# The sums behind a norm move from GpSimd to ScalarE, the power ahead of the copies, and the last output goes out in quarters

## The chip, the cores and the metric

One core of one Trainium2 chip. The metric is the device time of one execution in microseconds (us), the median of several; less is better. The core has five engines with queues of their own: TensorE (PE; its weight loads are shown apart as PEld), VectorE (DVE), ScalarE (ACT), GpSimd (POOL) and SyncE (SP), which here issues DMA transfers. Each engine takes its instructions strictly in the order of its own queue, and waits at an instruction until what it needs from other engines is there.

## The reference

Four decoder layers on 256 rows of 1024 columns, float32. In layers 0 and 3 the mixer is differential attention, in layer 1 stick-breaking attention, in layer 2 sliding-window attention. Each sublayer has a norm ahead of it and one behind it, and the one behind is what is changed here:

```python
def rms_norm(x, g):
    y = xf * lax.rsqrt(jnp.mean(xf * xf, axis=-1, keepdims=True) + NORM_EPS)
    return (y * g.astype(jnp.float32)).astype(x.dtype)
...
for i in range(DEPTH):
    hn = rms_norm(x, norm_gains[i, 0])
    m = mixer[i % 3](hn, ...)
    x = x + rms_norm(m, norm_gains[i, 1])
    hn = rms_norm(x, norm_gains[i, 2])
    x = x + rms_norm(swiglu(hn, ffn_w_gate[i], ffn_w_up[i], ffn_w_down[i]), norm_gains[i, 3])
```

## The kernel before

**Streams and weights.** The 256 rows are two streams, s = 0 (rows 0 to 127) and s = 1 (rows 128 to 255), each with its running state `x` of 128x1024 in on-chip memory. Both go through the same weights, stream 1 some units behind stream 0. A unit of weights, 128x1024, comes by DMA into `stage`, is rounded by ScalarE into `hi`, and VectorE takes the rest, `lo` = `stage` − `hi`. Activations are split alike (`xh` and `xl` behind a norm, `hTh` and `hTl` in the FFN), and each product is three matmuls: hi·high, lo·high and hi·low. FFN sums go to `mm_f` (gate and up) and, behind the down projection, to `acc_f`; the mixers' to `acc_a`, `acc_b` and `acc_c`.

**FFN hidden.** VectorE makes a block `h_f` of 128x256; GpSimd copies it into two planes of 16-bit words (`hp_f`); a DMA turns it (`hq_f`); GpSimd puts the words together again (`words`, L574 to L576, tile `hx_f`); from that ScalarE makes `hTh_f` and VectorE `hTl_f`, which the matmuls into `acc_f` take.

**Norms.** `post_norm` (L458) works on a sublayer's two sums of 128x512: ScalarE squares each and adds its columns up (`junk` with the sum in a column of `ssp`), GpSimd takes `u` = first sum + epsilon + second sum (one instruction, a TENSOR_SCALAR) and `r` = u to the power −0.5, both in `rstd_of` (L394), 128x1 each; VectorE makes `mg` = sum × gain, and then `x` += `mg` × `r` in two halves of 128x512. Tiles are named `_m` behind a mixer and `_e` behind an FFN. The next `pre_norm` (tiles `_q` ahead of an FFN, `_n` ahead of a mixer) has TensorE turn `x` in eight blocks of 128x128 (`tp_q`, `tp_n`: two tiles of four), from which ScalarE makes `xh` and VectorE `xl`; ScalarE also squares `x` (`junk_q`), and GpSimd makes `u_q` and `r_q`, from which VectorE makes `half` and `hsq` for the FFN. Behind the last layer SP writes each stream's `x` in two halves (L952 to L954).

**What sets the order.** `Emitter` (L39) runs the two streams as generators, with a clock of estimated matmul times and with delays that are written as `yield ("d", ns)`; that gives the order in which instructions are emitted. In the start phase each is pinned to that order on its engine (`Start`, L182); once that phase is over `.on` is False, and a scheduler of the framework puts each engine's instructions in an order of its own, by what they need and by its estimates of time. Only what goes through `tc.keep_in_program_order` stays where it was emitted: from then on the loads of weights and gains. Since the helper `run` at L182 issues nearly all instructions, the profile shows them under L182, and tiles tell them apart; only a few instructions issued directly have lines of their own.

Of the kernel before, what the change touches and what calls it, by code (L numbers as in the profile page):

```python
# [9 lines left out]
F32 = mybir.dt.float32  # L10
# [3 lines left out]
U16 = mybir.dt.uint16  # L14
AF = mybir.ActivationFunctionType
ALU = mybir.AluOpType
# [3 lines left out]
P = 128  # L20
# [3 lines left out]
EPS = 1e-6  # L24
# [134 lines left out]
def trunk_kernel(ctx, tc, x, positions, norm_gains, a_w_in, a_w_out, a_lambda, a_subln, b_w_in, b_w_out,  # L159
                 c_w_in, c_w_out, c_sinks, w_gate, w_up, w_down, out, depth=DEPTH):  # L160
    nc = tc.nc
# [4 lines left out]
    sm = ctx.enter_context(tc.tile_pool(name="sm", bufs=2))  # L166
# [20 lines left out]
    act, dve, pool, pe = (Start(e) for e in (nc.scalar, nc.vector, nc.gpsimd, nc.tensor))  # L187
# [87 lines left out]
    xs = [cst.tile([P, D], F32, name=f"x_{s}") for s in range(2)]  # L275
# [12 lines left out]
    mhalf = sm.tile([P, 8], F32, name="mhalf", bufs=1)  # L288
# [54 lines left out]
    def scalars():  # L343

        yield ("d", 9000)
        lsum = sm.tile([P, 4], F32, tag="lsum", name="lsum", bufs=1)
        lprod = wk.tile([P, 4, 64], F32, tag="t2k", name="lprod", bufs=TMP)
        lv = lam_in.rearrange("p i a b d -> p (i a) b d")
        pool.tensor_tensor(lprod, lv[:, :, 0, :], lv[:, :, 1, :], ALU.mult)
        dve.tensor_reduce(lsum, lprod, AX.X, ALU.add)  # L350
        act.activation(lsum, lsum, AF.Exp)
        for j in range(2):
            pool.tensor_scalar(nlam[:, j:j + 1], lsum[:, 2 * j + 1:2 * j + 2], lsum[:, 2 * j:2 * j + 1], -lam_init[j],
                                    ALU.subtract, ALU.add)
        tc.keep_in_program_order(pool.tensor_scalar(nsink, nsink, -1.0, None, ALU.mult))
        tps = bank("tp", 1, [P, 2], "tp_sub")
        nc.tensor.transpose(tps, subr, ident[:2, :2])
        for j in range(2):
            dve.tensor_scalar(gsub[:, j:j + 1], tps[:, j:j + 1], 1.0 - lam_init[j], None, ALU.mult)
# [31 lines left out]
        pe.transpose(o, i, ident)  # L391
        em.t += P * COLUMN_NS * 4

    def rstd_of(name, s, ss, more=EPS, extra=None):  # L394

        u = sm.tile([P, 1], F32, tag=f"u{s}", name=f"u_{name}")
        r = sm.tile([P, 1], F32, tag=f"r{s}", name=f"r_{name}", bufs=3)
        pool.tensor_scalar(u, ss, more, extra, ALU.add, *([ALU.add] if extra else []))
        pool.tensor_tensor(r, u, mhalf[:, 0:1], ALU.pow)
        return r  # L400

    def pre_norm(s, n, name):
# [24 lines left out]
        def rms():  # L427
            if n == 0:
                yield ("d", 2500)
                if s == 0:  # L430
                    sines(*angles)
                else:
                    act.on = dve.on = pool.on = False
            junk = wk.tile([P, D], BF16, tag="junk", name=f"junk_{name}", bufs=1)
            act.activation(junk, xs[s], AF.Square, scale=1.0 / 32, accum_out=ss)
            xn[2] = rstd_of(name, s, ss)
# [16 lines left out]
    def gain_of(i, n):  # L453
        if (i, n) not in gain_tiles:
            gain_tiles[i, n] = load_gain(i, n)
        return gain_tiles[i, n]

    def post_norm(s, acc, gain, name):  # L458
        ss = sm.tile([P, 2], F32, tag=f"ssp{s}", name=f"ssp_{name}")
        junk = wk.tile([P, D], BF16, tag="junk", name=f"junk_{name}", bufs=1)  # L460
        mg = [wk.tile([P, 512], F32, tag="t2k", name=f"mg_{name}{h}", bufs=TMP) for h in range(2)]
        for h in range(2):
            act.activation(junk[:, h * 512:(h + 1) * 512], acc[h], AF.Square, scale=1.0 / 32, accum_out=ss[:, h:h + 1])
        r = rstd_of(name, s, ss[:, 0:1], ss[:, 1:2], EPS)
        for h in range(2):
            dve.tensor_tensor(mg[h], acc[h], gain[:, h * 512:(h + 1) * 512], ALU.mult)
        for h in range(2):
            cs = slice(h * 512, (h + 1) * 512)
            dve.scalar_tensor_tensor(xs[s][:, cs], mg[h], r, xs[s][:, cs], ALU.mult, ALU.add)

    def rows_product(acc, ah, al, w, first, last):

# [11 lines left out]
    def out_proj(s, oT, name, last):  # L484

        acc = None
        for kt in range(KT):
            yield ("e", (name, "o", kt))
            w = yield ("w",)
            if acc is None:  # L490
                yield ("e", (name, "s", last))
                acc = [bank("acc", s, [P, 512], f"acc_{name}_{h}") for h in range(2)]
            oh, ol = (t[:, kt % 4, :] for t in oT[kt // 4])
            rows_product(acc, oh, ol, w, kt == 0, kt == KT - 1)
        return acc
# [77 lines left out]

    def words(dst, turned):  # L574

        pool.tensor_copy(dst.bitcast(U16).rearrange("p b (t w) -> p w b t", w=2), turned)  # L576

    def two_groups(s, name):
        return [[wk.tile([P, 4, P], F32R, tag=f"o{p}{s}", name=f"o{p}_{name}{g}") for p in "hl"] for g in range(2)]
# [298 lines left out]
    def ffn(s, i, xn):  # L878
# [19 lines left out]
        def turn(c, h):  # L898
            yield ("d", 2600)
            turned = by_dma(h, 2, f"{name}{c}")  # L900
            yield ("d", 4200)
            if c % 2 == 0:
                hT[c] = hT[c + 1] = [wk.tile([P, 4, P], F32R, tag=f"o{q}{s}", name=f"hT{q}_{name}{c}") for q in "hl"]
            t = wk.tile([P, 2, P], F32, tag="t2k", name=f"hx_{name}{c}", bufs=TMP)
            words(t, turned)
            split_rows(hT[c], slice(2 * (c % 2), 2 * (c % 2) + 2), t)
            em.set((name, "h", c))
# [23 lines left out]
    def stream(s):  # L931
        if s:
            yield ("d", 1500)
        for i in range(depth):
            kind = i % 3
            xn = pre_norm(s, 4 * i, f"n{i}{s}")
            yield ("d", 600)
            if i == 0 and s:
                em.spawn(scalars())
            oT, name = yield from (layer_a, layer_b, layer_c)[kind](s, i, xn)  # L940
            gain = gain_of(i, 1)
            acc = yield from out_proj(s, oT, name, (1, 1, 3)[kind])
            post_norm(s, acc, gain, f"m{i}{s}")
            yield ("d", 4000)
            gain = gain_of(i, 3)
            xn = pre_norm(s, 4 * i + 2, f"q{i}{s}")
            yield ("d", 600)
            acc = yield from ffn(s, i, xn)
            post_norm(s, acc, gain, f"e{i}{s}")
            if i < depth - 1:  # L950
                yield ("d", 4000)
        for h in range(2):  # L952
            cs = slice(h * 512, (h + 1) * 512)
            nc.sync.dma_start(out[0, s * P:(s + 1) * P, cs], xs[s][:, cs])  # L954

    em.run([stream(0), stream(1)])


# [23 lines left out]
```

## Time and profile before

| | |
|---|---|
| median of 3 runs | 1188.16 us (1187.87 to 1189.1) |
| the profiled execution | 1188.83 us, of which the span from its first to its last instruction is 1187.0 us |
| clock granted to TensorE | 0.997 of full speed |
| busy: TensorE, VectorE, ScalarE, GpSimd | 98%, 66%, 55%, 19% of the span |
| moved by DMA | 216.41 MB, 182 GB/s over the span |
| splits of weights | 378 `hi` of 1058 ns each, 378 `lo` of 1225 ns each |
| copies of FFN words | 80 `hp_f` of 1139 ns, 80 `hx_f` of 996 ns |
| powers behind a mixer (`r_m`) | 8 of 574 ns; their `u_m` 8 of 303 ns |

A row of the timeline gives the start, the duration, the engine, the line, the operation, output<-inputs with partitions x elements and type, and how many like it in a row; in brackets the idle time of the engine just ahead of it and what ended it. A row of the waits gives who waited for whom, the us in total, the times and the longest. A row of the groups gives the count behind x, the busy us in total, the mean ns of one, and then the idle time ahead of them. Consecutive rows of one engine may overlap by about 0.1 us, since the next instruction begins before the last one's result is complete.

### The profile page before, as it was taken

The page shows a single profiled execution, that of the slowest core. Times are in us where ns is not written, and L with a number is a line of the kernel's source. Part 1 is how long each engine was busy: PE and PEld are TensorE (multiplying, and loading weights), DVE is VectorE, ACT ScalarE, POOL GpSimd, SP SyncE. Part 2 cuts the span into 40 slices and gives each one's busy share as a digit, 9 for nine tenths or more (in the row PEclk, how much of TensorE's full clock was granted, in tenths as well). Part 3 has the DMA queues.
Part 4 walks back from the last instruction along what each step waited for, and adds up shares of the span by engine and source line. Part 5 has one row for each costly group of instructions (what it writes and reads, how often), then busy time and mean ns, then how long its engine had stood idle before and what let it go on. Part 6 is the DMA issues. An engine that isn't in the chain of part 4 may idle for free.

```text
span 1187.0 us, 16749 instructions
## 1 busy us (share of the span) xinstructions
PE 1165.1 (98%) x5869; PEld 957.0 (81%) x5869; DVE 782.7 (66%) x1213; ACT 655.3 (55%) x1209; POOL 224.5 (19%) x319
## 2 busy tenths in 40 slices
PE   8999999999999999999999999999999999999997
PEld 6787788888878878888888878888888788888886
DVE  6876665665847666665688666666586775766563
ACT  6665654444756655444477655444475565544441
POOL 5100132222200013222210013222210001322221
PEclk9999999999999999999999999999999999999999
DMA  7635467776743646777664346877765364577761
GB/s 261 210 125 176 131 193 220 208 221 198 221 135 126 213 129 190 205 221 208 199 197 160 108 129 195 213 211 214 205 198 155 131 192 150 177 212 212 208 194 40
DMA packets 183948, 216.41 MB, mean 182 GB/s; under 512 B 52788, under 2 KB 148152, under 8 KB 183864
## 3 DMA queue, kind: packets, MB, share of 16 engines
q1 hardware_dynamic: 183716, 215.28, 60.9%
q8 instruction: 46, 0.75, 0.3%
q14 instruction: 38, 0.31, 0.1%
q10 hardware_dynamic: 148, 0.07, 0.0%
HBM read 203.76 MB, written 1.05 MB: 173 GB/s over the span
## 4 chain that ended last, share of the span: by engine, by line
PE 89%; DVE 3%; ACT 2%; issue 2%; POOL 2%; DMA 2%; DVEq 0%; POOLq 0%; ACTq 0%; SPq 0%
PE mm_f L182 39%; PE acc_f L182 18%; PE acc_a L182 3%; PE mm_c L182 2%; PE acc_b L182 2%; PE acc_c L182 2%; PE sc_a L182 1%; DVE lo L182 1%; PE sc_c L182 1%; ACT hi L182 1%; PE sc_b L182 1%; DVE x L182 1%; DMA stage<-in_a_w_in_dram 1%; PE pv_a L182 1%; PE mm_a000k L182 1%
## 5 line engine op out<-in xcount | busy, mean ns | idle before, releaser
L182 DVE TENSOR_TENSOR lo<-stage,hi 128x1024 fp32r<-128x1024 f32 x378 | 459.5, 1225 | 163.0 <-ACT hi L182 160.6
L182 ACT ACTIVATE hi<-stage 128x1024 fp32r<-128x1024 f32 x378 | 396.0, 1058 | 168.0 <-PE mm_f L182 87.5
L182 PE MATMUL mm_f<-hi,xh_q 128*128 128x512 f32 x704 | 275.4, 391 | 1.5 <-ACT hi L182 1.5
L182 PE MATMUL mm_f<-lo,xh_q 128*128 128x512 f32 x704 | 274.0, 389 | 0.0
L182 PE MATMUL mm_f<-hi,xl_q 128*128 128x512 f32 x704 | 217.1, 389 | 0.4 <-DVE xl_q L182 0.4
L182 POOL COPY hp_f<-h_f 128x512 uint16<-128x512 uint16 x80 | 91.1, 1139 | 411.7 <-DVE h_f L182 404.9
L182 PEld LDWEIGHTS mm_f<-hi,xh_q 128*128 128x128 f32 x704 | 132.1, 188 | 30.2 <-ACT hi L182 3.2
L182 PEld LDWEIGHTS mm_f<-hi,xl_q 128*128 128x128 f32 x704 | 132.1, 188 | 28.9 <-DVE xl_q L182 1.3
L182 PEld LDWEIGHTS mm_f<-lo,xh_q 128*128 128x128 f32 x704 | 132.2, 188 | 27.1
L182 ACT ACTIVATE hTh_f<-hx_f 128x256 fp32r<-128x256 f32 x80 | 33.5, 419 | 160.8 <-POOL hx_f L182 160.8
L182 PE MATMUL acc_f<-hi,hTh_f 128*128 128x512 f32 x352 | 111.5, 392 | 1.2 <-ACT hTh_f L182 1.2
L182 PE MATMUL acc_f<-hi,hTl_f 128*128 128x512 f32 x352 | 109.8, 389 | 0.0
L182 PE MATMUL acc_f<-lo,hTh_f 128*128 128x512 f32 x352 | 109.8, 389 | 0.0
L182 DVE TENSOR_TENSOR hTl_f<-hx_f,hTh_f 128x256 fp32r<-128x256 f32 x80 | 33.9, 424 | 100.9 <-ACT hTh_f L182 100.9
L182 POOL COPY hx_f<-hq_f 128x512 uint16<-128x512 uint16 x80 | 79.7, 996 | 82.6 <-DMA hq_f<-hp_f 82.3
L182 ACT ACTIVATE t_f<-mm_f,half_f 128x256 f32<-128x256 f32 x88 | 41.6, 473 | 77.4 <-PE mm_f L182 77.4
L182 PEld LDWEIGHTS acc_f<-hi,hTh_f 128*128 128x128 f32 x352 | 65.8, 188 | 15.6 <-ACT hTh_f L182 2.4
L182 PEld LDWEIGHTS acc_f<-lo,hTh_f 128*128 128x128 f32 x352 | 66.1, 188 | 13.9
L182 PEld LDWEIGHTS acc_f<-hi,hTl_f 128*128 128x128 f32 x352 | 66.0, 188 | 13.8
L182 DVE SCALAR_TENSOR_TENSOR t_f<-t_f,mm_f 128x256 f32<-128x256 f32 x88 | 36.8, 419 | 34.1 <-ACT t_f L182 33.9
L182 DVE SCALAR_TENSOR_TENSOR h_f<-t_f,hsq_f,mm_f 128x256 f32<-128x256 f32 x88 | 42.3, 480 | 2.9
L182 ACT ACTIVATE e_a<-sc_a,nm_a 128x128 f32<-128x128 f32 (+1 forms) x64 | 26.1, 421 | 16.4 <-DVE nm_a L182 16.3
(589 smaller groups left out, 1557.5 us busy)
## 6 DMA issues: line engine op xcount, KB each, us to landing
stage<-in_ffn_w_gate_dram SPq DMA_DIRECT2D x176, 256.0 KB, 3.0
stage<-in_ffn_w_up_dram SPq DMA_DIRECT2D x176, 256.0 KB, 3.3
stage<-in_ffn_w_down_dram SPq DMA_DIRECT2D x88, 512.0 KB, 4.4
stage<-in_a_w_in_dram SPq DMA_DIRECT2D x48, 512.0 KB, 4.4
stage<-in_b_w_in_dram SPq DMA_DIRECT2D x24, 512.0 KB, 3.8
stage<-in_a_w_out_dram SPq DMA_DIRECT2D x16, 512.0 KB, 3.7
stage<-in_c_w_in_dram SPq DMA_DIRECT2D x10, 512.0 KB, 3.8
gain<-in_norm_gains_dram SPq DMA_DIRECT2D x8, 512.0 KB, 5.8
```

Source lines behind the costliest of these rows:

```text
L182: i = call(*args, **kw)
```

## The change

`rstd_of` now serves `pre_norm` alone. In `post_norm` GpSimd adds epsilon to the first sum, in place, as soon as that is there; ScalarE adds the two sums (an Identity activation of the second sum with the first as bias); GpSimd then takes only the power. The power and the copy in `words` are issued through `keep_in_program_order`, so on GpSimd these two kinds stay in the order in which they were emitted; GpSimd's other instructions are placed by the scheduler as before. In the last layer's FFN `post_norm` the four quarters of `x` are made one by one, and each stream's output goes out as 512, 256 and 256 columns.

```diff
@@ -391,11 +391,11 @@
         pe.transpose(o, i, ident)
         em.t += P * COLUMN_NS * 4
 
-    def rstd_of(name, s, ss, more=EPS, extra=None):
+    def rstd_of(name, s, ss):
 
         u = sm.tile([P, 1], F32, tag=f"u{s}", name=f"u_{name}")
         r = sm.tile([P, 1], F32, tag=f"r{s}", name=f"r_{name}", bufs=3)
-        pool.tensor_scalar(u, ss, more, extra, ALU.add, *([ALU.add] if extra else []))
+        pool.tensor_scalar(u, ss, EPS, None, ALU.add)
         pool.tensor_tensor(r, u, mhalf[:, 0:1], ALU.pow)
         return r
 
@@ -455,18 +455,24 @@
             gain_tiles[i, n] = load_gain(i, n)
         return gain_tiles[i, n]
 
-    def post_norm(s, acc, gain, name):
+    def post_norm(s, acc, gain, name, width=512):
         ss = sm.tile([P, 2], F32, tag=f"ssp{s}", name=f"ssp_{name}")
         junk = wk.tile([P, D], BF16, tag="junk", name=f"junk_{name}", bufs=1)
         mg = [wk.tile([P, 512], F32, tag="t2k", name=f"mg_{name}{h}", bufs=TMP) for h in range(2)]
+        u = sm.tile([P, 1], F32, tag=f"u{s}", name=f"u_{name}")
+        r = sm.tile([P, 1], F32, tag=f"r{s}", name=f"r_{name}", bufs=3)
         for h in range(2):
             act.activation(junk[:, h * 512:(h + 1) * 512], acc[h], AF.Square, scale=1.0 / 32, accum_out=ss[:, h:h + 1])
-        r = rstd_of(name, s, ss[:, 0:1], ss[:, 1:2], EPS)
+            if h == 0:
+                pool.tensor_scalar(ss[:, 0:1], ss[:, 0:1], EPS, None, ALU.add)
+        act.activation(u, ss[:, 1:2], AF.Identity, bias=ss[:, 0:1])
+        tc.keep_in_program_order(nc.gpsimd.tensor_tensor(r, u, mhalf[:, 0:1], ALU.pow))
         for h in range(2):
             dve.tensor_tensor(mg[h], acc[h], gain[:, h * 512:(h + 1) * 512], ALU.mult)
         for h in range(2):
-            cs = slice(h * 512, (h + 1) * 512)
-            dve.scalar_tensor_tensor(xs[s][:, cs], mg[h], r, xs[s][:, cs], ALU.mult, ALU.add)
+            for c in range(0, 512, width):
+                cs = slice(h * 512 + c, h * 512 + c + width)
+                dve.scalar_tensor_tensor(xs[s][:, cs], mg[h][:, c:c + width], r, xs[s][:, cs], ALU.mult, ALU.add)
 
     def rows_product(acc, ah, al, w, first, last):
 
@@ -573,7 +579,7 @@
 
     def words(dst, turned):
 
-        pool.tensor_copy(dst.bitcast(U16).rearrange("p b (t w) -> p w b t", w=2), turned)
+        tc.keep_in_program_order(nc.gpsimd.tensor_copy(dst.bitcast(U16).rearrange("p b (t w) -> p w b t", w=2), turned))
 
     def two_groups(s, name):
         return [[wk.tile([P, 4, P], F32R, tag=f"o{p}{s}", name=f"o{p}_{name}{g}") for p in "hl"] for g in range(2)]
@@ -946,11 +952,10 @@
             xn = pre_norm(s, 4 * i + 2, f"q{i}{s}")
             yield ("d", 600)
             acc = yield from ffn(s, i, xn)
-            post_norm(s, acc, gain, f"e{i}{s}")
+            post_norm(s, acc, gain, f"e{i}{s}", 256 if i == depth - 1 else 512)
             if i < depth - 1:
                 yield ("d", 4000)
-        for h in range(2):
-            cs = slice(h * 512, (h + 1) * 512)
+        for cs in (slice(0, 512), slice(512, 768), slice(768, 1024)):
             nc.sync.dma_start(out[0, s * P:(s + 1) * P, cs], xs[s][:, cs])
 
     em.run([stream(0), stream(1)])
```

The instructions of the two kernels stand in the same order up to small places around each `post_norm`. Tiles have a running number behind the name, which the change shifts by a few (`hi_1601` before is `hi_1603` after).

GpSimd in layer 0, from the FFN copies of stream 0 around the post-norm of stream 1's mixer (`_m`) to its next pre-norm (`_q`), before and then after:

```order
L182 COPY hp_f_1525<-h_f_1489 128x512
L182 TENSOR_SCALAR u_m_1573<-ssp_m_1567 128x1
L182 COPY hx_f_1583<-hq_f_1527 128x2x256
L182 TENSOR_TENSOR r_m_1574<-u_m_1573,mhalf 128x1
L182 COPY hp_f_1605<-h_f_1594 128x512
L182 TENSOR_SCALAR u_q_1640<-ss_q_1609 128x1
L182 TENSOR_TENSOR r_q_1641<-u_q_1640,mhalf 128x1
```

```order
L182 COPY hp_f_1526<-h_f_1490 128x512
L182 TENSOR_SCALAR ssp_m_1568<-ssp_m_1568 128x1
L469 TENSOR_TENSOR r_m_1573<-u_m_1572,mhalf 128x1
L582 COPY hx_f_1585<-hq_f_1528 128x2x256
L182 TENSOR_SCALAR u_q_1642<-ss_q_1611 128x1
L182 TENSOR_TENSOR r_q_1643<-u_q_1642,mhalf 128x1
L182 COPY hp_f_1607<-h_f_1596 128x512
```

The power has changed places with the copy `hx_f`, and `u_q` and `r_q` with the copy `hp_f`. ScalarE at the same place, before and after:

```order
L182 ACTIVATE junk_m_1568,ssp_m_1567<-acc_a_0_1349 128x512
L182 ACTIVATE junk_m_1568,ssp_m_1567<-acc_a_1_1350 128x512
L182 ACTIVATE hi_1601<-stage_1512 128x1024
L182 ACTIVATE hTh_f_1581<-hx_f_1583 128x256
L182 ACTIVATE t_f_1593<-mm_f_1493,half_f_1426 128x256
L182 ACTIVATE xh_q_1610<-tp_q_0_1612,gains 128x128 x4
L182 ACTIVATE xh_q_1610<-tp_q_1_1617,gains 128x128 x4
L182 ACTIVATE junk_q_1638,ss_q_1609<-x_111 128x1024
```

```order
L182 ACTIVATE junk_m_1569,ssp_m_1568<-acc_a_0_1350 128x512
L182 ACTIVATE junk_m_1569,ssp_m_1568<-acc_a_1_1351 128x512
L182 ACTIVATE hi_1603<-stage_1513 128x1024
L182 ACTIVATE u_m_1572<-ssp_m_1568 128x1
L182 ACTIVATE t_f_1595<-mm_f_1494,half_f_1427 128x256
L182 ACTIVATE hTh_f_1583<-hx_f_1585 128x256
L182 ACTIVATE junk_q_1640,ss_q_1611<-x_111 128x1024
L182 ACTIVATE xh_q_1612<-tp_q_0_1614,gains 128x128 x4
L182 ACTIVATE xh_q_1612<-tp_q_1_1619,gains 128x128 x4
```

The add stands behind the weight split `hi`, and not directly behind the squares; `hTh_f` has gone behind `t_f`, and `junk_q` ahead of `xh_q`. TensorE there, from the first matmul with that `hi` on, before and after:

```order
L182 MATMUL mm_f_1685<-hi_1601,xh_q_1386 128x512
L182 MATMUL acc_f_0_1655<-hi_1538,hTh_f_1581 128x512
L182 MATMUL tp_q_0_1612<-ident,x_111 128x128 x4
L182 MATMUL acc_f_1_1656<-hi_1538,hTh_f_1581 128x512
L182 MATMUL tp_q_1_1617<-ident,x_111 128x128 x4
L182 MATMUL mm_f_1648<-hi_1299,xh_q_1610 128x512
```

```order
L182 MATMUL mm_f_1687<-hi_1603,xh_q_1387 128x512
L182 MATMUL acc_f_0_1657<-hi_1539,hTh_f_1583 128x512
L182 MATMUL acc_f_1_1658<-hi_1539,hTh_f_1583 128x512
L182 MATMUL acc_f_0_1657<-lo_1540,hTh_f_1583 128x512
L182 MATMUL acc_f_1_1658<-lo_1540,hTh_f_1583 128x512
L182 MATMUL tp_q_0_1614<-ident,x_111 128x128 x4
L182 MATMUL mm_f_1687<-lo_1604,xh_q_1387 128x512
L182 MATMUL tp_q_1_1619<-ident,x_111 128x128 x4
```

Four matmuls that take `hTh_f` now stand ahead of the first turn of `x`, where one stood. On VectorE the subtraction that belongs to that `hi` (`lo_1604`, before `lo_1602`) has moved from behind `t_f` to between `mg_m` and `x`, and the `xl_q` behind `half` and `hsq`. The other layers show the same moves; in layer 2 the kernel before had even the first `acc_f` behind `tp_q_0`.

Behind the FFN of stream 1 in layer 1, ScalarE after the change (before, the same rows without `u_e`, which was GpSimd's):

```order
L182 ACTIVATE junk_e_5951,ssp_e_5950<-acc_f_0_4659 128x512
L182 ACTIVATE hi_6221<-stage_6076 128x1024
L182 ACTIVATE junk_e_5951,ssp_e_5950<-acc_f_1_4660 128x512
L182 ACTIVATE hi_6280<-stage_6094 128x1024
L182 ACTIVATE u_e_5954<-ssp_e_5950 128x1
L182 ACTIVATE hi_6334<-stage_6169 128x1024
L182 ACTIVATE xh_n_6029<-tp_n_0_6031,gains 128x128 x3
```

The add stands behind a `hi` here too, in layers 0 to 2; TensorE and VectorE keep their orders at these places. Behind the last layer it stands directly behind its squares.

## The prediction

> **What bounds the kernel now.** First the page: the span, the busy time and the chain that ended last.
>
> ```profile
> span 1187.0 us, 16749 instructions
> PE 1165.1 (98%) x5869; PEld 957.0 (81%) x5869; DVE 782.7 (66%) x1213; ACT 655.3 (55%) x1209; POOL 224.5 (19%) x319
> PE 89%; DVE 3%; ACT 2%; issue 2%; POOL 2%; DMA 2%; DVEq 0%; POOLq 0%; ACTq 0%; SPq 0%
> ```
>
> TensorE sets the end: busy for 98% of the span, and 89% of the chain. The change touches no matmul, so it can only alter TensorE's pauses. Its waits, largest first, hold three groups that lie around a post-norm:
>
> ```profile
> PE tp_q L182 <- DVE x L182: 2.5, 4, 1.2
> PE mm_f L182 <- ACT hi L182: 1.5, 4, 0.4
> PE acc_f L182 <- ACT hTh_f L182: 1.2, 4, 0.5
> ```
>
> Each occurs four times: once a layer, where stream 1 leaves its mixer. The timeline of layer 0 there, ScalarE, GpSimd, VectorE and TensorE in turn:
>
> ```profile
> 142.51 0.20 ACT L182 ACTIVATION_READ_ACCUMULATOR junk_m<-acc_a 128x1 f32 x1
> 142.60 1.05 ACT L182 ACTIVATE hi<-stage 128x1024 fp32r<-128x1024 f32 x1
> 143.95 0.42 ACT L182 ACTIVATE hTh_f<-hx_f 128x256 fp32r<-128x256 f32 x1 [0.31 <-POOL hx_f L182]
> 142.80 0.30 POOL L182 TENSOR_SCALAR u_m<-ssp_m 128x1 f32<-128x1 f32 x1 [7.75 <-ACT junk_m L182]
> 143.16 0.76 POOL L182 COPY hx_f<-hq_f 128x512 uint16<-128x512 uint16 x1
> 143.85 0.57 POOL L182 TENSOR_TENSOR r_m<-u_m,mhalf 128x1 f32<-128x1 f32 x1
> 144.46 1.41 DVE L182 SCALAR_TENSOR_TENSOR x<-mg_m,r_m,x 128x512 f32<-128x512 f32 x2 [1.04 <-POOL r_m L182]
> 143.70 0.49 PE L182 MATMUL mm_f<-hi,xh_q 128*128 128x512 f32 x1 [0.37 <-ACT hi L182]
> 144.42 0.50 PE L182 MATMUL acc_f<-hi,hTh_f 128*128 128x512 f32 x1 [0.23 <-ACT hTh_f L182]
> 145.36 0.63 PE L182 MATMUL tp_q<-ident,x 128*128 128x128 f32 x4 [0.43 <-DVE x L182]
> ```
>
> The power `r_m` stands behind `hx_f` on GpSimd. So `hTh_f` frees the first `acc_f` early (144.42) and `x` comes late: TensorE waits for each. In layer 2 only the second wait is left:
>
> ```profile
> 708.38 0.57 POOL L182 TENSOR_TENSOR r_m<-u_m,mhalf 128x1 f32<-128x1 f32 x1
> 709.88 0.63 PE L182 MATMUL tp_q<-ident,x 128*128 128x128 f32 x4 [1.16 <-DVE x L182]
> ```
>
> **Post-norm after the mixer, stream 1.** By the order of the changed kernel three things move at this place. ScalarE's add `u_m` stands behind `hi`; `r_m`, now pinned, stands ahead of `hx_f` and must wait for `u_m`; and VectorE's `lo` of that `hi` stands ahead of `x`. Queued behind the new wait on GpSimd is `hx_f`, behind it `hTh_f`, behind that four `acc_f`. TensorE now does these four before `tp_q`, where one stood before.
>
> Step by step in layer 0. `hi` ends at 142.60 + 1.05 = 143.65. The add on ScalarE is a kind that this kernel has only in neighbours:
>
> ```profile
> L182 ACT ACTIVATE es_c<-es_c 128x4 f32<-128x4 f32 x8 | 1.7, 215 | 0.0
> ```
>
> I take 0.215, begun 0.1 before the recorded end of `hi` (`hi` itself began 0.11 before the accumulator read ended): it ends at 143.77, or 143.87 if it waits for that end. GpSimd takes up work 0.09 after ScalarE (accumulator read end 142.71, `u_m` 142.80), so a free power would begin at 143.86. But `lo` begins as `mm_f` did, 0.05 after `hi`, at 143.70. What a `lo` does to GpSimd, two places show; the last row is the same small operation left alone:
>
> ```profile
> 320.14 3.49 DVE L182 TENSOR_TENSOR lo<-stage,hi 128x1024 fp32r<-128x1024 f32 x3
> 322.10 1.60 POOL L182 TENSOR_SCALAR u_n<-ss_n 128x1 f32<-128x1 f32 x1 [3.46 <-ACT junk_n L182]
> 204.46 1.23 DVE L182 TENSOR_TENSOR lo<-stage,hi 128x1024 fp32r<-128x1024 f32 x1 [0.53 <-ACT hi L182]
> 204.82 1.49 POOL L182 COPY hx_f<-hq_f 128x512 uint16<-128x512 uint16 x1 [1.79 <-DMA hq_f<-hp_f]
> L182 POOL TENSOR_SCALAR u_q<-ss_q 128x1 f32<-128x1 f32 x8 | 1.8, 223 | 10.3 <-ACT junk_q L182 10.2
> ```
>
> A 0.22 add takes 1.60 and ends 0.07 after its `lo` (323.63); a 0.76 copy takes 1.49 and ends 0.62 after its `lo` (205.69). Both begin inside a `lo` and finish after it, each 0.14 to 0.15 short of a full duration. So `r_m`, begun at 143.86 inside the `lo` of 143.70 to 144.93, ends at 144.93 + 0.57 − 0.15 = 145.35. No row shows a power begun inside a `lo`. An operation already begun isn't held:
>
> ```profile
> 309.98 0.57 POOL L182 TENSOR_TENSOR r_n<-u_n,mhalf 128x1 f32<-128x1 f32 x1
> 310.03 1.22 DVE L182 TENSOR_TENSOR lo<-stage,hi 128x1024 fp32r<-128x1024 f32 x1
> ```
>
> That power began 0.05 before the `lo` and took its usual 0.57; ours begins 0.16 after. The bounds for it are thus not held at all (ends 144.43) and begun only when `lo` is over (145.50). I take 145.35, by the two held rows, the same pair of engines.
>
> [...]
>
> On from 145.35: `hx_f` begins 0.07 before that (as `r_m` did behind it), 145.28, ends 146.04; `hTh_f` 146.07 to 146.49 (0.03 behind, as before); first `acc_f` 0.05 later, **146.54 instead of 144.42**. `x` begins at 145.39, and its first half is done by 146.1, while four `acc_f` of 0.227 each run to 147.45: the wait of `tp_q` is covered. The net: before, the work behind `tp_q` and one `acc_f` began at 145.36; now it is 146.54 + 0.23 = 146.77, **+1.41**. Layers 1 and 3 repeat the pattern: 3 × 1.41 = 4.2. Layer 2 (shifted by 708.38 − 143.85 = 564.53) has `acc_f` at 711.07, where `tp_q` began at 709.88: +1.19. Sum **+5.4**.
>
> Stream 1's `xh_q` goes behind `junk_q`, and `xl_q` behind `half`, `hsq`. By the same sums `xl_q` is ready about 0.3 before its matmul, so I cost it at nothing; without that cover, up to 0.2 a place. `hp_f` moves behind `r_q`, 1.3 later, about as much as TensorE itself: nothing. While `x` runs, `hx_f` may be slowed; its group mean bounds that:
>
> ```profile
> L182 POOL COPY hx_f<-hq_f 128x512 uint16<-128x512 uint16 x80 | 79.7, 996 | 82.6 <-DMA hq_f<-hp_f 82.3
> ```
>
> 996 against 760 ns is up to 0.24 a place, kept for the upper end. I take nothing: `hx_f` starts before `x`. GpSimd's early add of the epsilon lies beside the second square. Stream 0's post-norms have `u` directly behind the squares, and TensorE has no wait there: nothing either way.
>
> **Post-norm after the FFN, stream 1.** Here `u_e` stands behind one `hi`, while VectorE's order is as before. The three places, a row of the first, the others with their chains:
>
> ```profile
> 321.44 0.81 PE L182 MATMUL tp_n<-ident,x 128*128 128x128 f32 x6
> 617.64 2.13 ACT L182 ACTIVATE hi<-stage 128x1024 fp32r<-128x1024 f32 x2
> 618.23 0.57 POOL L182 TENSOR_TENSOR r_e<-u_e,mhalf 128x1 f32<-128x1 f32 x1
> 619.79 0.60 PE L182 MATMUL tp_n<-ident,x 128*128 128x128 f32 x4
> 884.63 1.42 DVE L182 SCALAR_TENSOR_TENSOR x<-mg_e,r_e,x 128x512 f32<-128x512 f32 x2 [0.36 <-POOL r_e L182]
> 889.52 0.69 DVE L182 TENSOR_TENSOR t_a300q<-t_a300q 128x512 f32<-128x512 f32 x1
> 890.37 0.60 PE L182 MATMUL tt_a300q<-ident,t_a300q 128*128 128x128 f32 x4
> ```
>
> Between layers 1 and 2 the first `hi` ends near 618.70, `u_e` near 618.82, so the power begins at 618.91 instead of 618.23, +0.68; `x` follows by as much, and `tp_n`, which began right after its first half, by **+0.6**. Between layers 2 and 3 the same delay goes through `x` and a VectorE that is not idle up to the `t_a300q` for which `tt_a300q` comes 0.16 after its end: **+0.6**, after a tenth of slack. Between layers 0 and 1, `x` is done near 320.2 (the `lo` behind it, shown above, begins at 320.14) and its `tp_n` begins at 321.44, more slack than that: nothing. Sum +1.2; bounds 0 (all found to be slack) and 1.4.
>
> **The end.** Here nothing covers anything:
>
> ```profile
> 1180.96 0.19 ACT L182 ACTIVATION_READ_ACCUMULATOR junk_e<-acc_f 128x1 f32 x1
> 1181.63 0.56 POOL L182 TENSOR_TENSOR r_e<-u_e,mhalf 128x1 f32<-128x1 f32 x1
> 1182.23 1.41 DVE L182 SCALAR_TENSOR_TENSOR x<-mg_e,r_e,x 128x512 f32<-128x512 f32 x2 [0.35 <-POOL r_e L182]
> out_dram<-x SPq DMA_DIRECT2D x4, 256.0 KB, 2.0
> L182 DVE SCALAR_TENSOR_TENSOR t_f<-t_f,mm_f 128x256 f32<-128x256 f32 x88 | 36.8, 419 | 34.1 <-ACT t_f L182 33.9
> ```
>
> From the read's end at 1181.15 the power began 0.48 later. With the add on ScalarE it is 0.21 to 0.36: −0.12 to −0.27. Four quarters of `x` instead of two halves cost more starts; the nearest row of 128x256, 0.42 each, would give 4 × 0.42 − 1.41 = +0.27 with none beside another, and I take half, +0.14, since halves follow each other without a gap. The last store is 128 instead of 256 KB, behind two others in the queue. Net −0.1 (−0.3 to +0.2).
>
> **Sum.** 5.4 + 1.2 − 0.1 = +6.5 on the profiled execution's 1188.83 (its span is 1187.0, 1.83 lie around it): 1195.3. The median of the runs is 0.67 below that execution, so **1194.7**.
>
> **Rivals.** *The power isn't held by `lo`* (for it: no power is seen held; against it: two other GpSimd operations are). Then `r_m` ends at 144.43, `hTh_f` at 145.57, `acc_f` begins at 145.62: 145.85 − 145.36 = +0.49 three times, and 710.15 − 709.88 = +0.27 in layer 2, 1.7; with 1.2 and −0.1, +2.8: 1191.0. *The delays are slack*: the same with the FFN places worth nothing, +1.6: 1189.8, or less if pauses further on take it up. For it: TensorE pauses at other places too; against it: at 98% busy it has little to take up. *Faster*: the add gets to ScalarE before `hi`, so that the change does what it says and the power comes straight behind the squares. Then `r_m` runs from about 142.92 to 143.49, `hx_f` to 144.18, `acc_f` begins at 144.68, the rest at 144.91 instead of 145.36: −0.45 three times, and 709.21 − 709.88 = −0.67 in layer 2; with −0.13 at two FFN places and −0.1 at the end, −2.4: 1185.8. The point from which it decides: the add must be over before `lo` begins at 143.70; ScalarE works in its order, in which `hi` is ahead, and `hi` has no wait there that could let it by. That speaks strongly against it.
>
> **How the numbers follow.** Forecast 0.62; power not held 0.20; slack 0.12; faster 0.06. About 0.2%, 2.4 us, is what a measurement of this kernel tells from no change: faster lies below 1185.8, slower above 1190.5. The last rival straddles the lower bound, so faster has 0.05; slack and the low part of the second rival give the same 0.14; slower has 0.81. The range: below, to 1190.5, which takes in the second rival; above, the forecast with the unknown costs of four places, 0.15 (power begun after `lo`), 0.24 (`hx_f` slowed) and 0.2 (`xl_q` late), 2.4 together, and the upper end of the last stores, 0.3: 1194.7 + 2.4 + 0.3 = 1197.4.
>
> **What would show it.** Right: TensorE's wait of `acc_f` for `hTh_f` grows from 1.2 to about 10 us over four places (0.23 + 2.12 each, and 2.6 in layer 2), that of `tp_q` for `x` is gone; `r_m` of stream 1 takes about 1.5 us instead of 0.57, ending 0.4 behind a `lo`; new waits of about 0.6 stand at `tp_n` after layer 1 and at `tt_a300q`. The second rival shows `r_m` at 0.57 inside a `lo`. The third shows `u_m` ahead of `hi` in ScalarE's timeline. Wrong in another way I would be if `x` were the later one at `tp_q`, or if new waits stood at `xl_q`.

## The result, and the profile after

| | before | after |
|---|---|---|
| median, first runs beside each other | 1188.32 us (4 runs, 1187.87 to 1189.1) | 1200.28 us (4 runs, 1199.24 to 1201.2) |
| ratio of the times | | 1.0101 (1.0089 to 1.0113) |
| median, both once more in one session | 1188.72 us (15 runs) | 1201.16 us (5 runs), ratio 1.0102 (1.0088 to 1.0116) |
| the profiled execution, and its span | 1188.83 us, 1187.0 us | 1201.2 us, 1199.4 us |

One of endonly's 11 runs below, and one of the 27 of the kernel before beside it, was in a slow state (1660.83 and 1945.32 us, at granted clocks of 0.655 and 0.557); the ratios leave these two out.

Slower by 12 us, where 6.5 was forecast, and outside the range. The page of the changed kernel, the span, the busy time and the chain:

```profile
span 1199.4 us, 16772 instructions
PE 1169.6 (98%) x5869; PEld 960.1 (80%) x5869; DVE 785.1 (65%) x1217; ACT 658.6 (55%) x1225; POOL 226.8 (19%) x319
PE 86%; DVE 4%; ACT 3%; DMA 2%; issue 2%; POOL 2%; POOLq 0%; DVEq 0%; ACTq 0%; SPq 0%
```

As many matmuls as before, and yet 4.5 us more of TensorE's busy time: they didn't only wait longer, some ran longer. TensorE's waits after the change:

```profile
PE acc_f L182 <- ACT hTh_f L182: 7.5, 4, 2.4
PE acc_f L182 <- DVE x L182: 2.3, 1, 2.3
...
PE mm_f L182 <- ACT hi L182: 1.5, 4, 0.4
...
PE tp_n L182 <- DVE x L182: 0.5, 1, 0.5
...
PE tt_a300q L182 <- DVE t_a300q L182: 0.4, 1, 0.4
```

`tp_q` for `x` is gone; `acc_f` now waits 9.8 us in all, about what the prediction named. The timeline of layer 0 behind stream 1's mixer, ScalarE, GpSimd, VectorE and TensorE in turn (this execution was about 2.0 us ahead of the one before here, see below):

```profile
140.63 1.05 ACT L182 ACTIVATE hi<-stage 128x1024 fp32r<-128x1024 f32 x1
141.57 0.28 ACT L182 ACTIVATE u_m<-ssp_m 128x1 f32<-128x1 f32 x1
...
144.11 0.42 ACT L182 ACTIVATE hTh_f<-hx_f 128x256 fp32r<-128x256 f32 x1 [1.89 <-POOL hx_f L582]
141.94 1.43 POOL L469 TENSOR_TENSOR r_m<-u_m,mhalf 128x1 f32<-128x1 f32 x1 [1.52 <-ACT u_m L182]
143.33 0.75 POOL L582 COPY hx_f<-hq_f 128x512 uint16<-128x512 uint16 x1
141.71 1.23 DVE L182 TENSOR_TENSOR lo<-stage,hi 128x1024 fp32r<-128x1024 f32 x1 [0.26 <-ACT hi L182]
143.41 1.82 DVE L182 SCALAR_TENSOR_TENSOR x<-mg_m,r_m,x 128x512 f32<-128x512 f32 x2 [0.47 <-POOL r_m L469]
141.73 0.49 PE L182 MATMUL mm_f<-hi,xh_q 128*128 128x512 f32 x1 [0.37 <-ACT hi L182]
144.58 1.22 PE L182 MATMUL acc_f<-hi,hTh_f 128*128 128x512 f32 x2 [2.35 <-ACT hTh_f L182]
145.60 1.05 PE L182 MATMUL acc_f<-lo,hTh_f 128*128 128x512 f32 x2
146.45 1.06 PE L182 MATMUL tp_q<-ident,x 128*128 128x128 f32 x4
```

The power begins 0.23 behind `lo`, takes 1.43 instead of 0.57 and ends 0.43 behind the end of `lo` (142.94), as forecast; the pause of `acc_f` is 2.35, as forecast. What the forecast doesn't have is in the last three rows. Two matmuls from 145.60 to 146.45 are 0.43 each, where the rows before show 0.227. TensorE runs at half speed, until 150.39. The table of windows, 10 us from the four pauses on (the columns are TensorE, its loads, VectorE, ScalarE and GpSimd, each with its busy time and count, then the clock granted to TensorE, the DMA share and GB/s):

```profile
142.00:152.00 10.00, 7.65 (x26) 6.05 (x26) 6.66 (x16) 4.08 (x12) 4.20 (x6) 0.66 0.24 73
445.00:455.00 10.00, 7.66 (x31) 6.11 (x32) 6.82 (x16) 5.17 (x14) 4.25 (x6) 0.83 0.26 73
714.00:724.00 10.00, 7.47 (x29) 5.91 (x30) 6.58 (x16) 4.95 (x15) 4.26 (x6) 0.83 0.33 95
1018.00:1028.00 10.00, 7.65 (x31) 6.20 (x31) 6.57 (x16) 5.02 (x14) 4.12 (x6) 0.83 0.25 73
```

The kernel before had a granted clock of 1.00 at all four places. The same view, cut to where the clock is 0.50 from end to end:

```profile
143.56:150.39 6.83, 5.81 (x18) 4.75 (x19) 4.84 (x13) 3.85 (x11) 1.87 (x4) 0.50 0.09 19
447.35:450.76 3.41, 2.93 (x9) 2.44 (x10) 2.37 (x6) 1.57 (x3) 0.93 (x3) 0.50 0.00 0
717.00:720.41 3.41, 3.39 (x11) 2.72 (x12) 1.73 (x5) 1.58 (x4) 1.37 (x3) 0.50 0.00 0
1020.79:1024.20 3.41, 3.41 (x14) 2.77 (x12) 2.00 (x6) 2.13 (x6) 1.35 (x3) 0.50 0.00 0
```

TensorE worked at half speed for 5.81 + 2.93 + 3.39 + 3.41 = 15.5 us. Half of that, 7.8 us, is what full speed would have saved; in the rest of these stretches it still paused.

**How the loss is counted by place.** The same matmul is looked up in both timelines; its shift behind a place less its shift ahead of it is what the place costs. In layer 0 the `mm_f` that waits for `hi` moved from 143.70 to 141.73, −1.97, and behind the place the shift is +2.2: 4.2 us. All the runs of this study, profiled execution against the profiled execution before, in us (m0 to m3: behind stream 1's mixer in layers 0 to 3; e0 to e2: behind its FFN; mixers: inside them, between these places; the FFNs in between never changed by over 0.1):

```
           start   m0     m1     m2     m3     e0     e1     e2   mixers
after      -2.05   4.19   2.80   2.81   3.03   0.19   0.83   0.80   0.1
again       0.12   1.49   3.08   2.87   3.01   1.10   0.80   1.03   0.0
fill8      -1.62   2.01   1.98   2.15   1.97   0.28   1.11   0.90  -0.1
mold       -1.49  -0.08  -0.08  -0.24  -0.11   0.43   0.81   0.77   0.1
eold       -1.15   2.94   1.47   2.84   1.43   0.17   0.02   0.11  -0.1
nolo       -0.14   0.69   0.69   0.45   2.14   1.85   1.67   1.33   3.0
nolom      -1.57   0.69   0.68   0.47   2.22   0.68   1.03   1.00   0.0
uhead      -0.37  -0.03  -0.07  -0.26  -0.05   0.65   0.83   0.09   3.6
uheadm      0.20  -0.05  -0.06  -0.26  -0.07   0.18   1.17   0.70  -0.1
pinonly    -1.40  -0.09  -0.11  -0.25  -0.14  -0.26   0.01   0.09  -0.1
endonly    -1.61   0.01   0.00   0.00  -0.05  -0.02   0.00   0.03   0.0
d2500      -0.30  -1.22  -1.21  -1.39  -1.23   1.50   0.50   0.27   3.8
hx0        -0.86  -1.17  -1.21  -1.41  -1.23   0.50   0.04  -0.04  -0.1
```

The first 60 us differ by up to 2 us between executions, whatever the kernel: `endonly`, which touches nothing there, has −1.61. They are no part of the change, and medians are needed beside this table.

### The profile page after: what moved, and what is told of

It reads as the page before. It is cut to its first block, busy times and chain, and to the rows that moved or that the text cites. A ratio compares the mean times of both kernels' runs of the same rounds, so it can differ in the third digit from the quotient of the medians.

```text
span 1199.4 us, 16772 instructions
## 1 busy us (share of the span) xinstructions
PE 1169.6 (98%) x5869; PEld 960.1 (80%) x5869; DVE 785.1 (65%) x1217; ACT 658.6 (55%) x1225; POOL 226.8 (19%) x319
## 3 DMA queue, kind: packets, MB, share of 16 engines
HBM read 203.76 MB, written 1.05 MB: 171 GB/s over the span
## 4 chain that ended last, share of the span: by engine, by line
PE 86%; DVE 4%; ACT 3%; DMA 2%; issue 2%; POOL 2%; POOLq 0%; DVEq 0%; ACTq 0%; SPq 0%
PE mm_f L182 39%; PE acc_f L182 18%; PE acc_a L182 3%; PE mm_c L182 2%; PE acc_c L182 2%; PE acc_b L182 2%; DVE lo L182 2%; PE sc_a L182 1%; ACT hi L182 1%; DVE x L182 1%; PE sc_c L182 1%; PE sc_b L182 1%; PE tp_q L182 1%; DMA stage<-in_a_w_in_dram 1%; PE pv_a L182 1%
```

## The experiments

The theories, as their expectations name them. A: `lo` holds the power, the pause of TensorE grows to 2.35, and a pause of this length halves the clock. B: the slow matmuls come from the new order, not from the pause. C: ScalarE's add costs by its place at `hi`, held or not. D: the power ahead of the copies costs by itself. E: the add costs at every norm. F: with the add directly behind its squares the change is faster. G: an earlier copy holds GpSimd up elsewhere. The edits are against the changed kernel where nothing else is said.

**The pause filled (fill8).**

```diff
+        if fill.pop("due", False):
+            o = bank("tp", 1, [P, 512], f"fill_{u}")
+            for _ in range(8):
+                pe.matmul(o, hi[:, 0:P], hi[:, 512:1024], start=True, stop=True)
         return hi, lo
```

> The changed kernel with eight matmuls of 128x512 added at each of the four places behind stream 1's mixer. They read the new hi, nobody reads their result, and they take about 1.8 us of TensorE's pause there; the waits of the other engines stay as they are. Theory A: TensorE's clock is halved because TensorE has nothing to do for 2.35 us, and that is 7.4 us of the loss. Then the half-speed stretches behind these places are gone, the pause left is about 1.0, and the median is near 1193.8 (1192.5 to 1195), one real matmul a place (0.23) having been pushed out of the pause. Theory B: the matmuls are slow for a reason of the new order (what they read, which banks they write), not for the pause. Then they stay at half speed and the median stays at 1199 to 1201.

Measured: 1198.46 us (4 runs), ratio 1.0083 (1.0069 to 1.0097). The windows of this run, at the same four places:

```profile
142.00:152.00 10.00, 9.16 (x42) 7.00 (x43) 8.00 (x17) 5.26 (x15) 4.64 (x6) 1.00 0.24 71
443.00:453.00 10.00, 9.02 (x41) 6.92 (x42) 8.00 (x17) 5.42 (x15) 4.53 (x6) 1.00 0.28 77
711.00:721.00 10.00, 8.53 (x40) 6.13 (x39) 7.44 (x18) 6.22 (x16) 4.27 (x6) 1.00 0.30 84
1013.00:1023.00 10.00, 8.88 (x41) 6.42 (x40) 8.09 (x18) 6.78 (x18) 3.71 (x6) 1.00 0.25 67
```

The clock is 1.00 at all four places, with the same waits of the other engines and eight more matmuls: with the pause filled it wasn't halved. One more thing differs, though. In this run's trace TensorE has one `acc_f` ahead of the first `tp_q` at these places, as in the kernel before, where the changed kernel has four. So this run alone doesn't rule out theory B; the next ones do.

The expected time was missed by 4.7. The 7.4 came from the first profile, which lost most to half speed of the three profiles with such pauses, and it was taken off a median. And behind the mixers the table still gives 8.1 (against 12.8 and 10.5), where 5.4 of waits and the pushed-out matmul (4 × 0.23) would be 6.3. The other 1.8 belong to this run's own order on TensorE; where they arise was not followed up.

**The changed kernel again (again).** No edit.

> The changed kernel once more, as the base for the others on this chip: 1199 to 1201.5. Theory A: half-speed stretches behind the four pauses again, of different lengths than in the first profile, because what halves the clock doesn't start with the kernel. Theory B (something of the order): the same lengths again, 5.7, 3.1, 3.1 and 2.9.

Measured: 1201.16 us. The windows:

```profile
144.00:154.00 10.00, 7.64 (x37) 6.12 (x38) 7.91 (x17) 5.60 (x15) 4.26 (x6) 1.00 0.27 75
446.00:456.00 10.00, 7.78 (x31) 6.46 (x32) 6.50 (x17) 4.92 (x12) 3.15 (x6) 0.83 0.28 55
```

In layer 0 the pause is 2.36 again, and the clock stays full; layers 2 and 3 are at 0.83 as well. The table has the price: 1.49 at the place that kept its clock, 2.9 to 3.1 at the other three. Layer 0, where TensorE worked 5.8 us at half speed in the first profile, has none here, with TensorE's matmuls in the same order. So the order by itself doesn't slow them, and B falls; lengths that differ between executions of one program speak for A.

**Which norms (mold, eold).** GpSimd adds both sums behind the mixers only (mold, here), or behind the FFNs only (eold, with "e" for "m").

```diff
-            if h == 0:
+            if h == 0 and name[0] != "m":
 ...
-        act.activation(u, ss[:, 1:2], AF.Identity, bias=ss[:, 0:1])
+        if name[0] == "m":
+            pool.tensor_scalar(u, ss[:, 0:1], ss[:, 1:2], EPS, ALU.add, ALU.add)
+        else:
+            act.activation(u, ss[:, 1:2], AF.Identity, bias=ss[:, 0:1])
```

> The changed kernel, but with GpSimd adding both sums behind the mixers as before; the add on ScalarE only behind the FFNs, the pins and the end as in the change. Theory A (the places behind the mixers carry the loss): behind the mixers as with the pins alone, about -0.5 in all; behind the FFNs +1.8 and the end -0.2: 1189.7 (1188.7 to 1191), no half-speed stretch behind a mixer. Theory E (ScalarE's add costs at every norm, the FFNs' too): 1193 or more.

> The changed kernel, but with GpSimd adding both sums behind the FFNs, the last one too; the add on ScalarE only behind the mixers. Theory A: the loss behind the FFNs (+1.8 by the profile of the change) goes and the end loses 0.1 to 0.2: 1198.6 (1197.6 to 1199.6). Theory E: half of the loss goes, 1194.

Measured: mold 1189.49 us (11 runs), ratio 1.0014 (1.0005 to 1.0023); eold 1197.85 us (5 runs), 1.0080 (1.0067 to 1.0093). As A has it: without the add behind the mixers 11.7 of the 12.4 us are gone; without it behind the FFNs 3.3. E, which expected 1193 or more and then 1194, falls. In eold's profile layers 1 and 3 kept their clock at pauses of 2.35 and cost 1.47 and 1.43; layers 0 and 2, halved for 3.23 and 3.41 us of TensorE's work, cost 2.94 and 2.84.

**Without the hold (nolo, nolom).** The next `lo` is queued behind `x`: at every post-norm (nolo), or behind stream 1's mixers alone (nolom, here).

```diff
+    def queue_behind(what, ins):
+        if what in behind:
+            tc.add_manual_dep(ins.ins, behind.pop(what).ins.name, ...)
 ...
-        dve.tensor_tensor(lo, t, hi.bitcast(F32), ALU.subtract)
+        queue_behind("x", dve.tensor_tensor(lo, t, hi.bitcast(F32), ALU.subtract))
 ...
+                if s and name[0] == "m":
+                    behind["x"] = i
```

> The changed kernel with one rule added: the subtraction lo of a newly split weight stands behind the x of the post-norm emitted before it on VectorE, so that no lo runs while the power does. The add still stands behind hi. Theory A (lo holds the power, and the long pause halves the clock): stream 1's r_m takes 0.57 again, the pause of TensorE there is 1.4 to 1.5, too short to halve the clock; +0.3 a place behind the mixers, +1.8 behind the FFNs as in the changed kernel, -0.2 at the end: median 1191 (1189.5 to 1192.5). Theory C (the add behind hi costs by itself, with or without lo): still 1196 or more.

> The changed kernel with the first lo that is split behind stream 1's post-norm of the mixer queued behind its x on VectorE, at these four places alone (the earlier form did it at every post-norm, and lost between 1 and 3.5 us behind each FFN, where it held the weights back). The add stays behind hi. Theory A: r_m takes 0.57, TensorE pauses 1.6 us, at most one place at half speed; +0.6 a place by two places of the earlier form, +1.8 behind the FFNs, -0.2 at the end: 1192.6 (1191.3 to 1194). Theory C (the add behind hi costs the most of it, held or not): 1197 or more.

Measured: nolo 1199.82 us, nolom 1195.33 us, ratio 1.0061 (1.0047 to 1.0075). Both lie above what was expected. In nolo the rule caught the splits behind FFNs and inside mixers too; the table shows 4.9 and 3.0 us there, and the run decides nothing. In nolom the timeline of layer 0 has, on GpSimd, VectorE and TensorE:

```profile
142.27 0.58 POOL L476 TENSOR_TENSOR r_m<-u_m,mhalf 128x1 f32<-128x1 f32 x1 [1.52 <-ACT u_m L182]
142.81 0.76 POOL L591 COPY hx_f<-hq_f 128x512 uint16<-128x512 uint16 x1
142.89 1.83 DVE L182 SCALAR_TENSOR_TENSOR x<-mg_m,r_m,x 128x512 f32<-128x512 f32 x2 [1.10 <-POOL r_m L476]
144.20 0.63 PE L182 MATMUL tp_q<-ident,x 128*128 128x128 f32 x4 [1.64 <-DVE x L182]
```

The power takes 0.58, and the place costs 0.69 instead of 1.49: the hold by `lo` is 0.8 us a place, and it lengthens the pause from 1.64 to 2.35 (TensorE has `tp_q` ahead of `acc_f` here). What is left at the places that kept their clock, 0.5 to 0.7, is where C is right. But the copy begins at 142.81, ahead of `x`, and now `x` takes 1.83 instead of 1.41. And in layer 3 a pause of 1.64 was followed by 3.4 us at half speed, and cost 2.22: a pause of this length can be enough, though in three of four places it wasn't. That is 1.6 of the 2.7 us above A's expectation; the FFN norms have most of the rest, 2.7 instead of 1.8.

**The add ahead of hi (uhead, uheadm).** The same device, with `hi` queued behind the add: at every post-norm, or behind stream 1's mixers alone.

```diff
-        act.activation(hi, t, AF.Copy)
+        queue_behind("u", act.activation(hi, t, AF.Copy))
```

> The changed kernel with one rule added: a weight's split hi stands behind the last ScalarE add emitted before it, so the add stands directly behind its squares. Theory A (the place of the add is what costs): r_m begins about 0.2 behind the squares and is not held, x comes 0.8 to 0.9 earlier than in the kernel before, acc_f 0.5 later, hi 0.2 later; -0.6 a place behind the mixers, about -0.1 behind two FFNs, -0.2 at the end: median 1186 (1184.5 to 1187.5), TensorE at full clock. Theory C (an add on ScalarE ahead of hi only moves the loss to hi and to TensorE's wait for it): 1188 to 1190.

> The changed kernel with the add ahead of hi behind stream 1's mixers only (the earlier form held back weights behind the FFNs and inside mixers, where the rule met splits that should have run earlier). Theory A, by the four places of the earlier form, which lost nothing (-0.03, -0.07, -0.26, -0.05): no pause long enough to halve the clock; behind the FFNs +1.8 to 2.9 as in the change, end -0.2: 1190.5 (1189.3 to 1192). Theory F (with the add in that place the change is faster than before, as its two freed instructions on GpSimd say): 1187 or less.

Measured: uhead 1192.55 us (5 runs), uheadm 1190.65 us (11 runs), ratio 1.0015 (1.0006 to 1.0024). uhead missed A's 1186: it again caught splits that should have run earlier (3.6 us inside the mixers), and the four places gained 0.4 together, where 2.4 were expected. uheadm is where A put it by those places, and F falls: with the add in the place that the change's code suggests, the four places gain 0.44 together. From uhead's timeline of layer 0:

```profile
142.74 0.19 ACT L182 ACTIVATION_READ_ACCUMULATOR junk_m<-acc_a 128x1 f32 x1
143.02 0.29 ACT L182 ACTIVATE u_m<-ssp_m 128x1 f32<-128x1 f32 x1
143.22 1.04 ACT L182 ACTIVATE hi<-stage 128x1024 fp32r<-128x1024 f32 x1
143.40 0.58 POOL L476 TENSOR_TENSOR r_m<-u_m,mhalf 128x1 f32<-128x1 f32 x1 [0.78 <-ACT u_m L182]
143.93 0.76 POOL L589 COPY hx_f<-hq_f 128x512 uint16<-128x512 uint16 x1
144.01 1.83 DVE L182 SCALAR_TENSOR_TENSOR x<-mg_m,r_m,x 128x512 f32<-128x512 f32 x2 [0.36 <-POOL r_m L476]
```

The add must wait 0.09 for the sum of its own engine, takes 0.29, and puts `hi` 0.29 behind the read's end instead of 0.11 ahead of it. `r_m` begins 0.47 behind the read's end; with both sums on GpSimd it takes the same: read's end, 0.09, 0.30, 0.08. The add on ScalarE saves nothing even there.

**The pins alone, the end alone (pinonly, endonly), on the kernel before.**

```diff
-        pool.tensor_tensor(r, u, mhalf[:, 0:1], ALU.pow)
+        i = nc.gpsimd.tensor_tensor(r, u, mhalf[:, 0:1], ALU.pow)
+        if extra is not None or pool.on:
+            tc.keep_in_program_order(i)
```

> The kernel before with the two pins alone: the power ahead of the copy hx on GpSimd, the sum of both squares still GpSimd's, the output as before. Theory A: r_m about 0.7 earlier, hx 0.5 later; acc_f begins at 144.94 in layer 0 and tp_q 0.2 earlier than before, 0.4 in layer 2: median 1187.3 (1186.3 to 1188.4), r_m at 0.57. Theory D (the power ahead of the copies costs by itself, since hTh comes late): +0.5 a place, 1190.3.

> The kernel before with the last x in quarters and the output in 512, 256 and 256 columns, nothing else. All theories: within 0.3 of the kernel before, 1188.6 (1188.0 to 1189.2); in the profile the last x begins when it did, takes 0.1 to 0.3 longer, and the last transfer of 128 KB lands 0.2 to 0.4 earlier behind its x.

Measured: pinonly 1187.96 us (11 runs), ratio 0.9997 (0.9988 to 1.0006); endonly 1188.62 us (11 runs), 0.9998 (0.9989 to 1.0007). (pinonly also pins the copies, as the change does; endonly is the part of the change's diff on widths and slices.) Neither can be told from no change, and D, which expected +0.5 a place, falls. By the table the pins gain 0.6 at the four places, where 1.0 was expected; `x` then runs beside `hx_f`, as in uhead's timeline above. The last store of 128 KB took as long as one of 256 KB (median times to landing of the two):

```profile
out_dram<-x SPq DMA_DIRECT2D x2, 256.0 KB, 2.0
out_dram<-x SPq DMA_DIRECT2D x4, 128.0 KB, 2.0
```

**The copy out of the way (d2500, hx0), on the kernel before.** GpSimd sat idle for 7.75 us ahead of `u_m`, and the transfer of the block for `hx_f` was issued at 135.07 and took 2.6 to land, long before `u_m` at 142.80; the copy came late only because it was emitted late.

```diff
-            yield ("d", 4200)
+            yield ("d", 2500 if s == 0 and c == 0 else 4200)
```

In d2500 the number stands without the condition, and also in the same line of differential attention, which its expectation leaves out.

> The kernel before with one number changed: the copy that puts a turned FFN block together is emitted 2500 instead of 4200 estimated ns behind its transfer, so that hx_f stands ahead of u_m and r_m on GpSimd, which sat idle for 7 us there while the block was already in. Theory A (what counts at these places is that neither hTh nor x waits for the other on GpSimd): acc_f for hTh waits no more, r_m comes 0.7 earlier, four acc_f fill the pause that x leaves: -1.2 a place, 1183.8 (1182.8 to 1186). Theory G (a copy that waits for its transfer at other places holds GpSimd up, and gives it back there): 1188 or more.

> The kernel before with the earlier emission only for the first FFN block of stream 0, the one whose copy stands between u_m and r_m at the four places behind stream 1's mixers; the other 76 copies stay where they were. Theory A: the four places gain what they gained with all copies earlier (-1.22, -1.21, -1.39 and -1.23 by the profile), and nothing is given back behind the FFNs and inside the mixers, where other copies were: -5.05, 1183.6 (1182.8 to 1184.8). Theory G: the copy itself is what holds other work up there, and half or more of it is given back: 1186 or more.

Measured: d2500 1189.82 us, ratio 1.0009 (0.9999 to 1.0020); hx0 **1183.30 us** (5 runs, 1182.17 to 1184.05) against 1188.02, ratio 0.9957 (0.9944 to 0.9971). In d2500 the four places gain 5.05, and the mixers (3.8) and FFN norms (2.3) give 6.1 back; whether the other copies or the line of differential attention cost this, no run tells. In hx0 the places gain 5.02 and 0.5 is given back, so this copy by itself isn't what G says. Its timeline of layer 0, GpSimd, VectorE, TensorE:

```profile
141.90 0.30 POOL L182 TENSOR_SCALAR u_m<-ssp_m 128x1 f32<-128x1 f32 x1 [3.29 <-ACT junk_m L182]
142.29 0.57 POOL L182 TENSOR_TENSOR r_m<-u_m,mhalf 128x1 f32<-128x1 f32 x1
142.89 1.41 DVE L182 SCALAR_TENSOR_TENSOR x<-mg_m,r_m,x 128x512 f32<-128x512 f32 x2 [0.36 <-POOL r_m L182]
142.28 0.61 PE L182 MATMUL acc_f<-hi,hTh_f 128*128 128x512 f32 x2
142.73 0.61 PE L182 MATMUL acc_f<-lo,hTh_f 128*128 128x512 f32 x2
143.70 0.66 PE L182 MATMUL tp_q<-ident,x 128*128 128x128 f32 x4 [0.35 <-DVE x L182]
```

The power directly behind the sum, `x` undisturbed, and four `acc_f` that wait for nobody in what was a pause. It is faster than both kernels.

## Why the prediction was wrong

Right in sign and in the waits behind the mixers, and too small, since the sum lacked a term. Its steps in turn:

- **The order, the hold, the pause: right.** `u_m` behind `hi`, `r_m` inside `lo`, 1.43 us (forecast 1.49, from the two held rows), and a pause of 2.35 (0.23 + 2.12). The rivals "not held" and "faster" have no place in any of these rows.
- **The waits behind the mixers, "+1.41", three times, and "+1.19": right.** Places that kept their clock cost 1.43, 1.47 and 1.49. Layer 2 was at half speed in all three profiles with such pauses; less half of its time at half speed it comes to 1.1 to 1.2. Added up like this, the waits of the four places are 5.1, 5.3 and 5.4 us (after, again, eold), and 5.4 was forecast. At these places TensorE waited for no `xl_q`, as costed.
- **The step that failed: the pause was priced at its length.** "The net" and "Sum +5.4" let TensorE go on at 0.227 a matmul behind a pause of 2.35. In 9 of the 12 pauses of that length (three profiles) it worked on at half speed for 2.9 to 5.8 us, and the place cost 2.8 to 4.2. Half of that time, the price of the halved clock, is 7.8 us in the first profile, 5.1 in the second and 3.3 in eold's. The sum has nothing for it, and no rival does.

The trace of before shows what was missed. The first row of its waits, in the start phase, was passed over because the change doesn't touch it:

```profile
PE tt_a000q L182 <- DVE t_a000q L182: 2.9, 1, 2.9
```

In its timeline, that wait and the rows behind it:

```profile
26.47 0.77 PE L182 MATMUL tt_a000q<-ident,t_a000q 128*128 128x128 f32 x4 [2.85 <-DVE t_a000q L182]
26.90 1.20 PE L182 MATMUL mm_a000k<-hi,xh_n 128*128 128x512 f32 x2
27.90 1.05 PE L182 MATMUL mm_a000k<-lo,xh_n 128*128 128x512 f32 x2
```

And the clock of that stretch in the windows:

```profile
26.88:30.29 3.41, 3.41 (x11) 2.73 (x10) 3.41 (x11) 3.39 (x4) 0.00 (x0) 0.50 0.85 256
```

Half speed for 3.4 us behind a pause of 2.85: 1.7 us of price, there to be read. With it at four places the sum would have been 6.5 + 4 × 1.7 = 13.3 on that execution, and with no halving 6.5; the measured 12 lies between, near the upper end.

- **Behind the FFNs, "+1.2": too small.** 1.8 in the first profile, 2.9 in the second. The delay itself was right (`r_e` 1.21 instead of 0.49 behind the read's end in layer 1), but the two places that were costed cost 0.8 to 1.0 each, and "layers 0 and 1 … nothing" cost 0.2 to 1.1. Why that place varies so was not tried.
- **The end, "−0.1": nothing that can be measured.** Stores of 128 KB land no sooner (2.0 us in endonly, as those of 256 KB). In the changed kernel's profile the power begins 0.47 behind the read's end, where it began 0.48 behind it before, so the add on ScalarE didn't save its 0.12 to 0.27; the four quarters of `x` take 1.67 instead of 1.41.

So the 12 us are, by the runs: 5 us of waits behind the mixers, as forecast, 2 to 3 behind the FFNs, where 1.2 was forecast, and about 5 of halved clock, where nothing was. The last fits the granted clock of the runs: 0.993 on average in nine runs of the changed kernel (0.991 to 0.995), 0.997 before, and 0.004 of 1199 us is 4.8.

## What to carry to other kernels

A pause of the matrix engine had two prices here: its length, 2.35 us, and the 2.9 to 5.8 us of work at half speed that followed 9 of 12 of them. Before a pause is lengthened, look in the same trace for what followed another of that length, even where the change doesn't reach; and look at more than one execution, since the same place had 5.8 us at half speed in one and none in another. And an instruction that "only" moves to an idle engine goes behind what is queued there (the add, behind a `hi` of 1.05 us); here the gain, 1183.30 us against 1188.02, was in moving nothing to another engine, but the copy that stood between a sum and its power to a time when its engine had nothing to do.

## What the runs showed of the hardware

- Half speed followed some of TensorE's short pauses and not others: those of 2.35 us in 9 of 12 places (after, again, eold), those of about 1.6 in 2 of 8 (nolo, nolom). In fill8, where TensorE idled for 0.84 to 1.47 us of the 10 us from each place on, it followed in none of 4. The same place of the same program kept its clock in one execution (again, layer 0) and had 5.8 us of work at half speed in another (after).
- Two traces show when the clock changed. In the changed kernel's first profile the half-speed stretches begin at 143.56, 447.35, 717.00 and 1020.79: 89, 79 and 89 times 3.413 us apart. Each lasts 3.41 us or twice that. In the kernel before, the clock fell at 26.88, rose at 30.29, and fell at 1184.00 behind the last matmul: once and 338 times 3.413 us apart. So in each of these executions the clock changed only at marks 3.41 us apart. Between the two marks ahead of a fall TensorE had idled for 1.71, 2.23, 2.69 and 2.62 us (after, layers 0 to 3), for 2.85 in the start phase of before, and for all of the 3.41 ahead of 1184.00. The other stretches between two marks that began at full speed, from 10 us on and up to the last matmul, had at most 1.47 idle in after and 1.19 in before, but for the one of after in which the last matmul lies, with 1.86; the clock stayed full behind all of them. So the idle time sorts them all but one (1.71 was followed by half speed, 1.86 wasn't); the ends of matmuls are modelled, which blurs it. The 1.47 belongs to a pause of 2.01 (after, 23.55 to 25.56), which a mark at 24.10 split in two. That the three pauses of 2.35 which kept their clock (again, layer 0; eold, layers 1 and 3) were split so is an estimate from this one; no run moved a pause on purpose.
- The power on GpSimd, begun 0.23 into a `lo` of VectorE, ended 0.43 behind it (1.43 instead of 0.57). It goes the other way as well: `x` begun 0.08 behind the start of a copy took 1.82 to 1.83 instead of 1.41.
- The add, a 128x1 activation with a tensor as bias, took 0.28 to 0.29 on ScalarE, and directly behind the squares it began only 0.09 after the read of their sum had ended, where a weight split begins 0.1 ahead of that.
